# Seven products in another order, the root inside the squared ReLU, x transposed in the first group, merges by early transfers

## The chip, the cores and the metric

The kernel runs on one core of a Trainium2 chip, in one launch. The time is the device time of that core in microseconds; it is given as the median of several runs, with the lowest and the highest. Beside it there is one execution taken with the profiler. The engines are named as the profile names them: PE is TensorE (matmuls; PEld its weight loads), DVE is VectorE, ACT is ScalarE, POOL is GpSimd, SP is SyncE. Each takes its instructions strictly in the order in which they stand in its queue. SP issues plain transfers; POOL issues transfers that add to what is already at their destination ("accumulating transfers").

## The reference

A trunk of two layers on x of 512 tokens by 1024 features, in float32. Each layer has an attention part (not touched by the change) and an MLP with a squared ReLU; at the end stands a last norm:

```python
for l in range(DEPTH):                      # DEPTH = 2
    h = rmsnorm(x, attn_norm[l])
    ...                                     # two kinds of attention, one output projection w_o
    x = x + einsum('bse,ed->bsd', mixed, w_o[l])
    h = rmsnorm(x, mlp_norm[l])             # x * rsqrt(mean(x^2) + 1e-6) * g
    u = square(relu(einsum('bsd,df->bsf', h, w_ff1[l])))     # 1024 -> 4096
    x = x + einsum('bsf,fd->bsd', u, w_ff2[l])               # 4096 -> 1024
return rmsnorm(x, final_norm)
```

The norm's factor is one number per token, so it may be applied to the product with `w_ff1` rather than to x; and since it is positive, it may be applied after the squared ReLU as its square, 1 / (mean(x^2) + eps), which needs no root.

## The kernel before

**Precision.** Every float32 operand is split into a high part (rounded to the matmul's format) and a low part (the rest). A product takes three matmuls: high x high, high x low, low x high (`three`, L281 to L283). ACT makes the high part (L116 for weights, L224 for activations), DVE the low part (L117, L225). Weights come in units of 512 KB; `_Weights` loads them (SP, L99), splits them some units ahead and hands them out. While a layer's MLP runs, four split units are held.

**Layout.** x lies transposed, as 8 chunks of 128 features by 512 tokens. `h_hi`, `h_lo` are x times the norm's gain, split (`make_h`, L228 and L229); the sum of squares over the features is gathered in `ssq` (L235, L238) during the output projection `wo`.

**The MLP** of a layer runs in four groups of 1024 hidden features. A group first makes eight blocks of 128 hidden features (tiles `f`, 24 matmuls each, into PSUM banks that rotate over five). `evict_u` takes each block out of PSUM: ReLU (L810), square (L811), splits and, for two blocks together (a "pair"), the differences that the second half needs (L816, L819). The work tiles F hold one pair at a time.

The second half of a group multiplies with `w_ff2`. Two halves of the tokens, two of the hidden features and two of the output columns make a 2x2 by 2x2 block product; it is done with seven products instead of eight (a Strassen scheme), named in `FORMS`: "11", "21", "x1", "22", "x2", "x3", "x4", in this order. Each takes 24 matmuls into two PSUM banks, and `gather` (L833, L835) adds the result to a tile of its own, `y[form]`, over the four groups. The left operand of a form is one of seven splits of a pair (`SIDE`): 0 to 2 are quarters of u, 3 to 6 differences. The right operands are sums of quarters of `w_ff2` ("11", "12", "21", "22"). They are made in three buffers per unit by transfers: `fetch` loads a quarter (SP, L777), `grow` adds another to it (POOL, L783) as soon as the form that used the buffer before has been split; "11" becomes x1, x2 and x4 in turn, and "21" is replaced by "12" and grown by "22" to x3 (L782).

**The ends.** In the last group the seven tiles are combined into the four quarters of the result. `merge` (L843) adds one tile to another by an accumulating transfer on POOL's queue, `join` (L840) does it on DVE. In layer 0, `back` (L872, L873) transposes the result chunk by chunk on PE, adds it to x, and makes the next layer's h; the first two blocks of the next projection (tiles `p`) follow at once, then `p1w0v`. In the last layer the result stays with tokens in rows, so x is transposed the other way (`turned`, L852) and added; then come the sums of squares for the last norm (`square`, L878), its factor (`root`, L883 and L884), the gains (`weigh`, L888, and L896) and the stores (L894, L896, L898).

**The norm's factor in the MLP.** At the head of the first group the sum over features is made (L929, L930), and its reciprocal is held per token in `r2` (L934). It is applied at the very end: `settle` scales what has been combined so far (L862 on ACT in layer 0; L858 on DVE in the last layer, together with x), and `add_to` (L866) adds each late product scaled. `rms_a` and `rms_b`, which the attention uses for its own norms, make the root and spread it over a tile: PE transposes and DVE sums (L248 to L251), POOL takes the power -1/2 (L259), DVE makes the high and the low diagonal (L260 to L266), PE multiplies them with ones (L274, L275), ACT copies the result into `rbc` (L276).

**The order.** The program is written down in one order, and a scheduler places the instructions of each engine by priority; waits are put in from what reads and writes what. The order of an engine's queue is thus fixed before the run. Places such as `(g, k, n) == (0, 0, 6)` say after which matmuls something is written.

## Time and profile before

| | |
|---|---|
| time, median of 3 runs | 1177.74 us (1174.94 to 1179.62) |
| profiled execution, its own time | 1172.68 us |
| its span, first to last instruction | 1170.9 us |
| granted TensorE clock, mean | 0.998 |
| PE busy | 1147.6 us (98%) |
| DVE busy | 813.1 us (69%) |
| ACT busy | 651.5 us (56%) |
| POOL busy | 212.7 us (18%) |
| moved by DMA | 170.11 MB |

The MLP of layer 0 begins near 249 us and gives way to the next layer near 577; that of the last layer begins near 829. Durations of matmuls overlap (they are pipelined), so the distance of two starts, 0.227 us for 512 columns, is what one costs. On DVE too an instruction begins some 0.08 us before the end of the one ahead. A wait is shown in square brackets: the idle time before the instruction and what ended it. A busy time over a window stands in the order PE, PEld, DVE, ACT, POOL, with the number of instructions, then the granted clock, the DMA engines' share and GB/s.

### The profile page before, as it was taken

The page shows a single profiled execution, that of the slowest core. Times are in us where ns is not written, and L with a number is a line of the kernel's source. Part 1 is how long each engine was busy: PE and PEld are TensorE (multiplying, and loading weights), DVE is VectorE, ACT ScalarE, POOL GpSimd, SP SyncE. Part 2 cuts the span into 40 slices and gives each one's busy share as a digit, 9 for nine tenths or more (in the row PEclk, how much of TensorE's full clock was granted, in tenths as well). Part 3 has the DMA queues.
Part 4 walks back from the last instruction along what each step waited for, and adds up shares of the span by engine and source line. Part 5 has one row for each costly group of instructions (what it writes and reads, how often), then busy time and mean ns, then how long its engine had stood idle before and what let it go on. Part 6 is the DMA issues. An engine that isn't in the chain of part 4 may idle for free.

```text
span 1170.9 us, 15335 instructions
## 1 busy us (share of the span) xinstructions
PE 1147.6 (98%) x5454; PEld 951.2 (81%) x5454; DVE 813.1 (69%) x1302; ACT 651.5 (56%) x1153; POOL 212.7 (18%) x282
## 2 busy tenths in 40 slices
PE   9999999999999999999899999999999999999996
PEld 6787888888888888888677878888888888888885
DVE  7888788765545746647778887877664466475568
ACT  6455666556656446455445555655666564554554
POOL 1222443130100101002012215331201010010021
PEclk9999999999999999999999999999999999999999
DMA  7555333255844936727416553432548357276185
GB/s 243 158 156 172 119 116 108 72 189 153 196 149 108 229 123 125 222 96 159 106 54 190 153 161 109 125 110 72 216 120 224 128 127 228 93 148 210 36 175 132
DMA packets 56860, 170.11 MB, mean 145 GB/s; under 512 B 7120, under 2 KB 8144, under 8 KB 56784
## 3 DMA queue, kind: packets, MB, share of 16 engines
q1 hardware_dynamic: 46416, 131.88, 34.0%
q0 software_dynamic: 10224, 37.23, 18.0%
q8 instruction: 43, 0.70, 0.2%
q14 instruction: 33, 0.27, 0.1%
q10 hardware_dynamic: 144, 0.02, 0.0%
HBM read 138.17 MB, written 2.10 MB: 120 GB/s over the span
## 4 chain that ended last, share of the span: by engine, by line
PE 86%; DVE 5%; DMA 2%; issue 2%; ACT 1%; POOL 0%; SPq 0%; POOLq 0%; DVEq 0%; ACTq 0%
PE f L283 10%; PE f L281 10%; PE f L282 10%; PE x L281 4%; PE x L283 4%; PE x L282 4%; PE wo L281 3%; PE wo L283 3%; PE wo L282 3%; DMA q<-in_w 2%; DVE wlo L117 1%; PE T1s L555 1%; PE T0s L555 1%; PE O0s L584 0%; PE O1s L584 0%
## 5 line engine op out<-in xcount | busy, mean ns | idle before, releaser
L117 DVE TENSOR_TENSOR wlo<-raw,whi 128x1024 fp32r<-128x1024 f32 (+1 forms) x132 | 157.0, 1193 | 95.6 <-ACT whi L116 95.0
L117 DVE TENSOR_TENSOR wlo<-q,whi 128x512 fp32r<-128x512 f32 x224 | 145.9, 687 | 108.6 <-ACT whi L116 108.1
L281 PE MATMUL f<-h_hi,whi 128*128 128x512 f32 x512 | 199.6, 390 | 0.0
L283 PE MATMUL f<-h_hi,wlo 128*128 128x512 f32 x512 | 199.3, 389 | 0.0
L282 PE MATMUL f<-h_lo,whi 128*128 128x512 f32 x512 | 199.2, 389 | 0.0
L116 ACT ACTIVATE whi<-q 128x512 fp32r<-128x512 f32 x224 | 129.4, 624 | 123.7 <-DMA q<-in_w 45.4
L116 ACT ACTIVATE whi<-raw 128x1024 fp32r<-128x1024 f32 (+1 forms) x132 | 133.9, 1019 | 111.7 <-PE f L282 55.0
L783 POOL DMA_DIRECT2D q<-in_w x64 | 56.0, 882 | 557.1 <-DVE wlo L117 471.3
L283 PEld LDWEIGHTS f<-h_hi,wlo 128*128 128x128 f32 x512 | 96.1, 188 | 20.1
L282 PEld LDWEIGHTS f<-h_lo,whi 128*128 128x128 f32 x512 | 96.1, 188 | 20.0
L281 PEld LDWEIGHTS f<-h_hi,whi 128*128 128x128 f32 x512 | 96.1, 188 | 19.7
L225 DVE TENSOR_TENSOR Al<-F,Ah 128x256 fp32r<-128x256 f32 (+2 forms) x96 | 74.8, 779 | 44.1 <-ACT Ah L224 44.0
L281 PE MATMUL x<-whi,Ah 128*128 128x512 f32 x256 | 100.0, 391 | 0.0
L282 PE MATMUL x<-wlo,Ah 128*128 128x512 f32 x256 | 99.8, 390 | 0.0
L283 PE MATMUL x<-whi,Al 128*128 128x512 f32 x256 | 99.7, 389 | 0.0
L224 ACT ACTIVATE Ah<-F 128x256 fp32r<-128x256 f32 (+2 forms) x96 | 67.6, 704 | 45.7 <-DVE F L819 43.7
L282 PEld LDWEIGHTS x<-wlo,Ah 128*128 128x128 f32 x256 | 48.1, 188 | 10.3 <-DVE wlo L117 0.5
L283 PEld LDWEIGHTS x<-whi,Al 128*128 128x128 f32 x256 | 48.1, 188 | 10.0
L281 PEld LDWEIGHTS x<-whi,Ah 128*128 128x128 f32 x256 | 48.1, 188 | 9.8
L810 ACT ACTIVATE F<-f 128x512 f32<-128x512 f32 x64 | 37.5, 587 | 10.8 <-DVE Al L225 5.4
L811 ACT ACTIVATE F<-F 128x512 f32<-128x512 f32 x64 | 40.4, 631 | 1.5
L228 ACT ACTIVATE h_hi<-x,g_all 128x512 fp32r<-128x512 f32 x32 | 22.5, 718 | 26.6 <-DVE x L692 13.8
(1059 smaller groups left out, 2566.5 us busy)
## 6 DMA issues: line engine op xcount, KB each, us to landing
raw<-in_w SPq DMA_DIRECT2D x126, 512.0 KB, 3.6
q<-in_w SPq DMA_DIRECT2D x64, 512.0 KB, 5.5
q<-in_w POOLq DMA_DIRECT2D x64, 512.0 KB, 5.9
x<-in_xT SPq DMA_DIRECT2D x8, 256.0 KB, 4.6
raw<-in_w SPq DMA_DIRECT2D x8, 128.0 KB, 4.5
yx<-y POOLq DMA_DIRECT2D x2, 512.0 KB, 8.0
y<-y POOLq DMA_DIRECT2D x2, 512.0 KB, 7.5
y<-yx POOLq DMA_DIRECT2D x2, 512.0 KB, 5.3
```

What stands on the lines that cost most here:

```text
L116: h = nc.scalar.activation(hi[:, a:b], raw[:, a:b], AF.Copy)
L117: self.last = h, nc.vector.tensor_tensor(out=lo[:, a:b], in0=raw[:, a:b], in1=hi[:, a:b].bitcast(F32), op=ALU.subtract)
L224: nc.scalar.activation(hi, src, AF.Copy)
L225: nc.vector.tensor_tensor(out=lo, in0=src, in1=hi.bitcast(F32), op=ALU.subtract)
L228: a = nc.scalar.activation(h_hi[:, c, :], x[:, c, :], AF.Copy, scale=g)
L281: nc.tensor.matmul(pt, ah, bh, start=first, stop=False)
L282: nc.tensor.matmul(pt, ah, bl, start=False, stop=False)
L283: nc.tensor.matmul(pt, al, bh, start=False, stop=last)
L555: nc.tensor.transpose(pt[:, off : off + P], u["w"][qi][:, kb * P : (kb + 1) * P], ident)
L783: nc.gpsimd.dma_start(t, quad(g, q, c), accum_op=ALU.add)
L810: nc.scalar.activation(t, pt, AF.Relu)
L811: nc.scalar.activation(t, t, AF.Square)
```

## The change

- The forms run in the order "11", "x3", "x1", "22", "x2", "21", "x4". The buffer that held "21" first and x3 later now holds x3 first: a group ahead, "12" is loaded and "22" added to it; once x3 is split, "21" is loaded over it.
- The norm's factor is made as a root by `rms_a` and `rms_b` in the first two blocks of the first group, into `rbc`. `evict_u` takes a block out of PSUM with one DVE instruction that does the ReLU and multiplies by `rbc`; ACT's ReLU goes. The first block is held back until the second has been multiplied. `column`, `settle` and `add_to` go.
- In the last layer six of the eight transposes of x (`forth`, formerly `turned`) are written into the tiles `y` in the first group, and the forms "21", "22" and "x4" add to them from the start. The other two stand in the form x2 of the last group.
- In the last group "11" is merged into x2 and 21 at once, x3 into x4, x1 into x3, x1 into 22, by five transfers; x2 is then joined to x3, x4 and 22 on DVE, for both layers alike. The places of `back`, `square`, `root`, `weigh` and `store` follow.

```diff
--- before.py
+++ after.py
...
-FORMS = ("11", "21", "x1", "22", "x2", "x3", "x4")
+FORMS = ("11", "x3", "x1", "22", "x2", "21", "x4")
...
                 W.raw[unit(g, form, c)] = kept[k][c]
-                nc.sync.dma_start(kept[k][c], quad(g, form, c))
-
-            def grow(g, form, q, c, over=None):
+                nc.sync.dma_start(kept[k][c], quad(g, "12" if form == "x3" else form, c))
+                if form == "x3":
+                    nc.gpsimd.dma_start(kept[k][c], quad(g, "22", c), accum_op=ALU.add)
+
+            def grow(g, form, q, c):
                 t = kept[HOME[form]][c]
-                if over:
-                    nc.sync.dma_start(t, quad(g, over, c))
-                nc.gpsimd.dma_start(t, quad(g, q, c), accum_op=ALU.add)
+                if q == form:
+                    nc.sync.dma_start(t, quad(g, q, c))
+                else:
+                    nc.gpsimd.dma_start(t, quad(g, q, c), accum_op=ALU.add)
...
                             ("11", grow, (g, "x1", "12", c)), ("x1", grow, (g, "x2", "22", c)),
-                            ("x2", grow, (g, "x4", "21", c)), ("21", grow, (g, "x3", "22", c, "12")),
-                            ("x4", fetch, (g + 1, "11", c)), ("x3", fetch, (g + 1, "21", c)),
+                            ("x2", grow, (g, "x4", "21", c)), ("x3", grow, (g, "21", "21", c)),
+                            ("x4", fetch, (g + 1, "11", c)), ("21", fetch, (g + 1, "x3", c)),
...
                             W.then.setdefault(unit(g, form, c), []).append(lambda fn=fn, args=args: fn(*args))
-            for form in ("11", "21", "22"):
+            for form in ("11", "x3", "22"):
             def evict_u(pt, g, k, forms):
...
                 t = F[:, 2 * which : 2 * which + 2, :].rearrange("p a t -> p (a t)")
-                nc.scalar.activation(t, pt, AF.Relu)
+                nc.vector.scalar_tensor_tensor(out=t, in0=pt, scalar=0.0, in1=rbc, op0=ALU.max, op1=ALU.mult)
...
                     split(hi[:, 0, :], lo[:, 0, :], F[:, 1, :])
...
-            fresh = set(FORMS)
-            home = {(1, 0): "21", (1, 1): "22", (0, 0): "x4", (0, 1): "z" if last else "x1"}
+            fresh = set(FORMS) - ({"21", "22", "x4"} if last else set())
+            home = {(1, 0): "21", (1, 1): "22", (0, 0): "x4", (0, 1): "x3"}
...
                 return y[home[(tb // 2, j)]][:, tb % 2, :]
...
-            def column(tb):
-                return r2[:, tb : tb + 1]
-
-            def turned(tb, j):
+            def forth(tb, j):
...
                     nc.tensor.transpose(pt[:, k * P : (k + 1) * P], x[:, 4 * j + k, tb * P : (tb + 1) * P], ident)
-                return pt
-
-            def settle(tb, j):
-                o = place(tb, j)
-                if last:
-                    nc.vector.scalar_tensor_tensor(
-                        out=o, in0=o, scalar=column(tb), in1=turned(tb, j), op0=ALU.mult,
-                        op1=ALU.subtract if j else ALU.add)
+                if (tb // 2, j) == (0, 1):
+                    nc.vector.tensor_sub(place(tb, j), place(tb, j), pt)
                 else:
-                    nc.scalar.activation(o, o, AF.Copy, scale=column(tb))
-
-            def add_to(tb, j, src):
-                o = place(tb, j)
-                nc.vector.scalar_tensor_tensor(
-                    out=o, in0=src, scalar=column(tb), in1=o, op0=ALU.mult, op1=ALU.add)
+                    nc.scalar.activation(place(tb, j), pt, AF.Copy, scale=-1.0 if j else 1.0)
...
-            r2 = fin[:, 0:4]
+            def diagonals():
+                f = fp.tile([P, 4, S], F32R, tag="F", name=f"diag{l}")
+                parts_ = iter((f[:, 0, :], f[:, 1, :]))
+                return lambda name: next(parts_)
+
...
                 end = g == GROUPS - 1
...
                     nc.scalar.activation(sin_t, sin_t, AF.Copy, scale=-math.sqrt(D))
+                waiting = []
...
                         if (g, k, n) == (0, 0, 6):
-                            ptr = bank("t", f"rs_m{l}")
-                            for j in range(4):
-                                nc.tensor.transpose(ptr[:, j * P : (j + 1) * P], ssq[:, j * P : (j + 1) * P], ident)
-                            nc.vector.tensor_reduce(
-                                out=r2, in_=ptr.rearrange("p (j f) -> p j f", j=4), axis=AX.X, op=ALU.add)
-                            nc.vector.tensor_scalar(
-                                out=r2, in0=r2, scalar1=1.0 / D, scalar2=EPS, op0=ALU.mult, op1=ALU.add)
-                            nc.vector.reciprocal(r2, r2)
-                    evict_u(pt, g, k, forms)
-                    if end and k in (2, 3):
-                        settle(k - 2, 0)
+                            dg = rms_a(ssq, 1.0 / D, rcol, f"m{l}", nc.vector, diagonals())
+                        if (g, k, n) == (0, 1, 4):
+                            rms_b(rbc, f"m{l}", dg)
+                    waiting.append((pt, k))
+                    if (g, k) == (0, 0):
+                        continue
+                    for one, i in waiting:
+                        evict_u(one, g, i, forms)
+                    waiting = []
+                    if last and g == 0 and k < 7:
+                        forth(*((2, 0), (3, 0), (2, 1), (3, 1), (0, 0), (1, 0))[k - 1])
...
                     work = [(c, i, r) for c in range(GP // 2) for i in range(2) for r in range(2)]
...
                               n == mine[0], n == mine[-1])
-                        if end and last and form == "x3" and n == 3:
-                            join("22", "x2")
-                            for tb in (2, 3):
-                                settle(tb, 1)
-                                square(tb, 1)
-                                root(tb)
-                                weigh(tb, 0)
+                        if end and last and form == "x2" and n in (1, 3):
+                            forth(n // 2, 1)
                         if tail and last and n == 3:
-                            add_to(0, 0, to[0])
+                            gather("x4", to, (0,))
                             square(0, 0)
-                            weigh(2, 1)
-                            weigh(3, 1)
                             root(0)
                             for tb in (2, 3):
-                                for j in range(2):
-                                    store(tb, j, True)
-                        if tail and not last and n == 5:
-                            for c_ in CAME[:2]:
+                                weigh(tb, 0)
+                                store(tb, 0, True)
+                                store(tb, 1, True)
+                        if tail and not last and n in (3, 5, 7):
+                            for c_ in ((4,), (5, 6), (7,))[n // 2 - 1]:
...
                         break
-                    if end and not last and form == "x3":
-                        for tb in (0, 1):
-                            add_to(tb, 1, to[tb])
...
                         merge("x2", "11")
-                    elif form == "21":
                         merge("21", "11")
+                    elif form == "x3":
+                        merge("x4", "x3")
+                    elif form == "x1":
+                        merge("x3", "x1")
                     elif form == "22":
                         merge("22", "x1")
-                        for tb in (2, 3):
-                            settle(tb, 0)
-                        if last:
-                            for tb in (2, 3):
-                                square(tb, 0)
-                            y["z"], t = (e.rearrange("p (a t) -> p a t", a=2) for e in kept[2])
-                            for tb in (0, 1):
-                                nc.scalar.activation(place(tb, 1), turned(tb, 1), AF.Copy, scale=-1.0)
-                                nc.scalar.activation(t[:, tb, :], y["x1"][:, tb, :], AF.Copy, scale=column(tb))
-                            y["t"] = t
-                            merge("z", "t")
                     elif form == "x2":
                         join("x3", "x2")
-                        if not last:
-                            join("x1", "x3")
-                            join("22", "x2")
-                            for tb in range(4):
-                                settle(tb, 1)
-                    elif form == "x3":
+                        join("x4", "x2")
+                        join("22", "x2")
                         if last:
                             for tb in (0, 1):
-                                add_to(tb, 1, y["x3"][:, tb, :])
                                 square(tb, 1)
-                        for tb in (0, 1):
-                            add_to(tb, 0, y["x3"][:, tb, :])
+                            for tb in (0, 1):
+                                weigh(tb, 1)
+                    elif form == "21" and last:
+                        for j in (1, 0):
+                            for tb in (2, 3):
+                                square(tb, j)
+                        for tb in (2, 3):
+                            root(tb)
+                            weigh(tb, 1)
             if last:
-                add_to(1, 0, to[1])
+                gather("x4", to, (1,))
                 square(1, 0)
                 store(0, 0, False)
-                weigh(0, 1)
                 store(0, 1, True)
-                weigh(1, 1)
...
                 store(1, 1, True)
...
                 pts = [bank("mm", f"p{l + 1}{i}") for i in range(2)]
-                for tb in (0, 1):
-                    add_to(tb, 0, to[tb])
-                for c in CAME[2:4]:
-                    back(c)
+                gather("x4", to)
```

## The prediction

> **What bounds the kernel now.** I read the page's parts 1 and 4, then busy time by stage, then TensorE's own waits.
>
> ```profile
> span 1170.9 us, 15335 instructions
> PE 1147.6 (98%) x5454; PEld 951.2 (81%) x5454; DVE 813.1 (69%) x1302; ACT 651.5 (56%) x1153; POOL 212.7 (18%) x282
> PE 86%; DVE 5%; DMA 2%; issue 2%; ACT 1%; POOL 0%; SPq 0%; POOLq 0%; DVEq 0%; ACTq 0%
> ...
> 252.00:333.00 81.00, 81.00 (x361) 67.06 (x360) 44.23 (x65) 51.03 (x80) 8.27 (x9) 1.00 0.72 206
> 496.00:577.00 81.00, 79.35 (x349) 64.89 (x348) 49.98 (x74) 43.78 (x70) 9.62 (x11) 1.00 0.54 122
> 577.00:600.00 23.00, 19.52 (x97) 15.10 (x98) 21.97 (x32) 11.74 (x18) 0.13 (x2) 1.00 0.17 60
> 1076.00:1171.00 95.00, 84.11 (x386) 69.23 (x384) 61.60 (x95) 49.12 (x86) 12.65 (x16) 0.98 0.50 115
> ...
> PE xT L852 <- DVE y L858: 2.6, 1, 2.6
> PE yT L872 <- DVE x L873: 1.9, 1, 1.9
> ```
>
> The window rows give, after the stretch, its length and the busy times of PE, PEld, DVE, ACT, POOL. TensorE is busy 81.00 of 81 us in an MLP group: nothing taken from another engine there is worth anything. In the MLPs time is lost in two places only, both at the end of a layer: 577 to 600 (and the 1.65 ahead of it), where DVE is busy 21.97 of 23 us, and the last group, where TensorE lacks 10.9 of 95 us, 8.2 of them behind its last matmul.
>
> **The change part by part.** The profiled execution took 1172.68 us, its span 1170.9; the median of the runs shown is 1177.74, 5.06 above. The sum is made against the former and carried over to the median.
>
> **The root at the head of each MLP (a cost).** The old reciprocal was needed late. Now rms_a and rms_b run in the first two blocks, and the two matmuls of rms_b stand in TensorE's order after five products of the second block.
>
> ```profile
> 256.51 0.69 DVE L930 TENSOR_REDUCE fin<-rs_m 128x4 f32<-128x512 f32 x1
> 258.29 0.39 PE L281 MATMUL f<-h_hi,whi 128*128 128x512 f32 x1
> 260.53 0.60 ACT L810 ACTIVATE F<-f 128x512 f32<-128x512 f32 x1 [2.69 <-PE f L283]
> 601.08 0.69 DVE L249 TENSOR_REDUCE ms<-rs_a 128x4 f32<-128x512 f32 x1 [0.99 <-PE rs_a L248]
> 602.06 1.04 POOL L259 TENSOR_TENSOR rcol<-ms,mhalf 128x4 f32<-128x4 f32 x1 [1.15 <-DVE ms L251]
> 604.05 0.69 DVE L266 TENSOR_TENSOR dgla<-edge,clo 128x512 fp32r<-128x512 f32 x1
> 608.85 0.59 ACT L276 COPY rbc<-rb_a 128x512 f32<-128x512 f32 x1 [4.39 <-PE rb_a L275]
> ```
>
> The same chain at the attention's head goes from reduction to second diagonal in 604.05 + 0.69 - 601.08 = 3.66 us. Here the reduction starts at 256.51 (the weight splits ahead of it on DVE are unchanged), so the diagonal is there at 260.17. TensorE, in order, arrives at 258.29 and goes on after the second matmul (0.23, the distance of two matmuls) at 260.4: +2.1 per layer, **+4.2** for two. The lower bound is 0.9, the four matmuls alone; the upper 6.7, if one more wide DVE instruction (1.23, as at 380.51 below) gets into each chain. The factor is then copied (0.59) by about 261.4, while the second block ends 2.1 after its old eviction at 260.53: the first pair is late only by TensorE's own shift. The power goes ahead of the accumulating transfers on POOL's queue; their weights are needed only after eight blocks of 24 matmuls.
>
> **The ReLU on DVE (nothing).**
>
> ```profile
> L810 ACT ACTIVATE F<-f 128x512 f32<-128x512 f32 x64 | 37.5, 587 | 10.8 <-DVE Al L225 5.4 <-PE f L283 5.4
> L413 DVE SCALAR_TENSOR_TENSOR t1s0q<-p1s0q,rbc x1: 692/692/692, 678.7 to 678.7; 128x512 f32<-128x512 f32 x1
> 374.57 0.39 PE L281 MATMUL 11010_3748<-whi,Ah 128*128 128x512 f32 x1
> 375.20 0.69 DVE L117 TENSOR_TENSOR wlo<-q,whi 128x512 fp32r<-128x512 f32 x1 [2.56 <-ACT whi L116]
> 380.51 1.23 DVE L225 TENSOR_TENSOR Al<-F,Ah 128x1024 fp32r<-128x1024 f32 x1
> ```
>
> ACT loses 37.5 us; DVE gains 64 x 0.69 = 44, 5.5 per group, and goes from 50 to 56 of 81 us. TensorE hides it. The tight place is the product now second, "x3": it needs the differences of the last pair, which "21" did not. Products take 24 matmuls, 5.44 us; the last pair of the second is wanted at 374.57 + 5.44 + 18 x 0.227 = 384.1. Its low part is ready at 380.51 + 1.23 = 381.7, and the new instruction falls into DVE's 2.56 idle ahead of it. Slack 2.4 us; with that cover gone, eight groups would pay each microsecond eight times.
>
> **Transposes of x (a cost).**
>
> ```profile
> 1153.48 1.04 PE L852 MATMUL xT<-edge,x 128*128 128x128 f32 x8
> 1154.27 0.47 PE L281 MATMUL x<-whi,Ah 128*128 128x512 f32 x1
> ```
>
> Eight take 0.79, 0.1 each. Six sets of four go into the last layer's first group, where TensorE has no room: +2.4. Two sets leave the last group's blocks: -0.8. **+1.6**, bounds 1.4 and 2.6 (four at 0.66 where they follow a wait).
>
> **The weights and the merges.** SP's queue keeps its order and count: "x3" and "21" change places. POOL's has two transfers more in layer 0, one more in layer 1, and the two accumulations for "x3" move into the group before.
>
> ```profile
> 546.05 0.86 POOL L783 DMA_DIRECT2D q<-in_w  x1 [1.59 <-DMA q<-in_w]
> 546.61 1.19 POOL L843 DMA_DIRECT2D yx<-y  x1
> 549.18 0.88 POOL L783 DMA_DIRECT2D q<-in_w  x1 [1.38 <-DVE y L835]
> 552.04 0.87 POOL L843 DMA_DIRECT2D y<-y  x1 [1.97 <-issue]
> 554.56 0.86 POOL L783 DMA_DIRECT2D q<-in_w  x1 [1.65 <-DVE yx L835]
> ...
> 543.21 0.39 PE L281 MATMUL 21030_5022<-whi,Ah 128*128 128x512 f32 x1
> ...
> 549.18 8.43 DMA q<-in_w
> 563.63 5.32 DMA q<-in_w
> ```
>
> A lone transfer lands 5.3 after its issue (last line); in a backlog one follows another at some 2.65 (issues at 549.18, 552.04, 554.56) and takes 8.43. The second accumulation for x2 lands at 549.18 + 8.43 = 557.6 now and about 557 then: two merges are ahead of it in place of one merge and x3's accumulation. From there, 2.65 each: x3 into x4 559.5; x4's first weights 562.2; x1 into x3, which on POOL waits until x3 into x4 has landed, 559.6 + 5.3 = 564.9; x4's second 567.5; x1 into 22, 570.2. DVE's order puts the three joins, and in layer 1 two subtractions of x ahead of them, in front of the second half of x4's last weight split. That half is done 2.7 after the last merge (a join and a half of it queued, then the half): 572.9. TensorE begins x4, the seventh product, at 543.21 + 5 x 5.44 = 570.4 and wants the half 18 matmuls on, at 574.5: slack 1.6. In layer 1 x4's halves of tokens come one after the other, so on the same clock it is wanted at 573.5, and two multiplications by the gain (1.2) are ahead of it too: done at 574.4, a wait of 0.9 that I expect to see there.
>
> [...]
>
> **The end of layer 0 (a gain).**
>
> ```profile
> 575.49 1.40 DVE L866 SCALAR_TENSOR_TENSOR yx<-x,fin,yx 128x512 f32<-128x512 f32 x2
> 576.81 1.27 DVE L835 TENSOR_TENSOR yx<-yx,x 128x512 f32<-128x512 f32 x2
> 592.73 3.88 DVE L238 TENSOR_TENSOR ssq<-ssq,spare 128x512 f32<-128x512 f32 x5 [0.29 <-ACT spare L237]
> 597.80 0.50 PE L283 MATMUL p1w0v<-h_hi,wlo 128*128 128x512 f32 x1 [1.17 <-DVE wlo L117]
> ```
>
> DVE is the bound there. Six scaled additions (L866) go, of which pairs start 576.81 - 575.49 = 1.32 apart: -4.0, and two plain ones of x4 take the place of two of x3 before. One more addition to `ssq` (0.78) now stands ahead of the split for which TensorE waits at 597.80. **-3.2**, bounds 0 (the joins come late) and -5.1 (all that TensorE lacks in the two windows, 1.65 + 3.48).
>
> **The end of the kernel (a gain).**
>
> ```profile
> 1145.02 0.66 PE L852 MATMUL xT<-edge,x 128*128 128x128 f32 x4 [2.61 <-DVE y L858]
> 1162.33 0.39 PE L283 MATMUL x<-whi,Al 128*128 128x512 f32 x1
> 1166.37 0.75 DVE L896 SCALAR_TENSOR_TENSOR yx<-yx,fin,cos_t 128x512 f32<-128x512 f32 x1 [0.66 <-POOL fin L884]
> ```
>
> The wait of 2.61 goes: the two sets left there find their banks free. But the last store comes 4.0 after the last matmul, off DVE's queue. On that, from x2's additions on, two L858 and six L866 go (8 x 0.66 = 5.3); one join of 1024 (1.14), two additions of x4 and two multiplications by the gain (4 x 0.6) come: **-1.8**. Bounds 0 and -3.8, the shift of TensorE's last matmul.
>
> Sum: 4.2 + 0 + 1.6 - 3.2 - 1.8 = +0.8: 1173.5 for the profiled execution, **1178.5** beside the median. 0.5%, 5.9 us, is about what a measurement can tell.
>
> **The rivals.**
> *Merges late (slower).* Five merges per layer instead of three or four, DVE waits for the last two, and the split of x4's weights stands behind them. For it: the queue is full in the rows above; POOL is blocked while x1 into x3 waits. Against: two accumulations leave this stretch. From 1.6 late it costs both layers; from 3.4 late it decides (1.8 in layer 0, 3.4 in layer 1, on top of +0.8: 6.0). Two transfers late, 5.3: 3.7 + 5.3 + 0.8 = +9.8, **1187.5**. Chance 0.2.
>
> *Both ends relieved (faster).* DVE had 21.97 of 23 us; without the scalings TensorE could run through: 4.2 + 1.6 - 5.1 - 3.8 = -3.1; with roots as early as their bound, -6.4: **1171.3**. Against it: 3.66 us of chain can't fit in 258.29 - 256.51. Chance 0.1.
>
> *Nothing hidden, nothing gained.* The second product waits for its differences and the new order costs what the ends give. From 2.4 late; at 3 late 8 x 0.6 = 4.8: 1183.3. Against it: the 2.56 idle. Chance 0.04.
>
> *The clock falls.*
>
> ```profile
> 1140.00:1150.00 10.00, 7.39 (x41) 6.01 (x40) 8.11 (x14) 6.91 (x15) 2.60 (x3) 1.00 0.93 173
> 1163.00:1171.00 8.00, 0.00 (x0) 0.00 (x0) 3.46 (x6) 2.85 (x6) 1.10 (x2) 0.76 0.51 197
> ```
>
> The granted clock (after POOL's column) stays 1.00 over an idle of 2.61 and is 0.76 over one of 8. My waits at the roots are 1.7; twice that, and then half speed for as long, would be 2 x 3.4 = +6.8 on the sum: 1185.3. Chance 0.03. [...]
>
> **How the numbers follow.** The forecast, within 0.5%, holds 0.63. Slower is merges 0.2 and clock 0.03; faster 0.1; the late differences lie inside. That leaves 0.67 for the same. The range, 1173 to 1187, leaves out most of the faster case and the worst of the merges; the likeliest case alone spans 1174 to 1183.
>
> **What the profile after would show.** TensorE waiting about 1.7 us at rms_b in both layers; no wait above 0.3 within groups; L813 64 times at 0.69; no ACT wait of 7 us on a transfer (L862 is gone) but DVE waits on merges in the last groups; the TensorE waits of 577 to 600 mostly gone; the last matmul some 3 us earlier against the start of its group, the last store about 2. Wrong I would be if the joins or the roots came a transfer later than reckoned, or if TensorE lost time in groups 1 to 3.

## The result, and the profile after

The changed kernel takes 1180.16 us (median of 13 runs, 1177.94 to 1182.32), the kernel before, run beside it, 1175.15 us (13 runs, 1173.54 to 1179.62). The ratio is 1.0038, its 95% interval 1.0027 to 1.0049: 4.5 us slower, a small but measured loss, inside the half per cent that I called no change. The forecast of 1178.5 lies close, but its sum does not: it stood on a median of 1177.74 of three runs, and said +0.8 where +4.5 was measured.

The profiled execution of the changed kernel took 1180.27 us, near its own median; that of the kernel before, 1172.68, lies 2.5 below its median. So the two profiles differ by 7.5 us in their spans. That is what is accounted for below; where part of the 2.5 comes from is shown with the experiments.

From the page of the changed kernel, span and busy time:

```profile
span 1178.4 us, 15339 instructions
PE 1152.0 (98%) x5458; PEld 953.3 (81%) x5458; DVE 852.4 (72%) x1367; ACT 611.0 (52%) x1079; POOL 219.8 (19%) x287
```

TensorE's busy time grew by 4.4 us for four more matmuls: some matmuls got longer. Its waits (total, times, longest), and busy time by stage (columns as before: PE, PEld, DVE, ACT, POOL, granted clock, DMA share, GB/s):

```profile
PE rb_m L274 <- DVE diag L264: 4.6, 2, 2.4
PE yT L861 <- DVE x L862: 2.4, 1, 2.4
...
PE x L282 <- DVE wlo L117: 0.9, 1, 0.9
```

```profile
252.00:333.00 81.00, 78.82 (x342) 64.55 (x342) 49.13 (x74) 44.24 (x70) 11.66 (x12) 0.98 0.74 196
833.00:915.00 82.00, 79.58 (x357) 65.18 (x356) 50.34 (x77) 45.21 (x73) 12.69 (x13) 0.98 0.67 181
333.00:415.00 82.00, 82.00 (x363) 67.92 (x362) 54.57 (x81) 39.13 (x59) 6.94 (x8) 1.00 0.61 157
577.00:600.00 23.00, 19.42 (x98) 14.91 (x96) 20.88 (x31) 11.48 (x18) 0.13 (x2) 1.00 0.15 46
```

The first groups of both MLPs, full at clock 1.00 before, now lack 2.2 and 2.4 us and run at 0.98; the second group (third line) is full as before. TensorE's timeline gives the stages: the first block, the first "11" of the first and of the last group, the transposes for the next norm (`rs_a`), the last matmul. First the changed kernel, then the one before.

```profile
248.64 0.39 PE L281 MATMUL f<-h_hi,whi 128*128 128x512 f32 x1
...
260.27 0.47 PE L274 MATMUL rb_m<-diag,ones_r 128*128 128x512 f32 x1 [2.14 <-DVE diag L264]
260.78 0.79 PE L275 MATMUL rb_m<-diag,ones_r 128*128 128x512 f32 x1
261.37 0.63 PE L281 MATMUL f<-h_hi,whi 128*128 128x512 f32 x1
261.80 0.63 PE L282 MATMUL f<-h_lo,whi 128*128 128x512 f32 x1
...
264.95 0.39 PE L282 MATMUL f<-h_lo,whi 128*128 128x512 f32 x1
265.17 0.39 PE L283 MATMUL f<-h_hi,wlo 128*128 128x512 f32 x1
...
297.38 0.39 PE L281 MATMUL 11000_3142<-whi,Ah 128*128 128x512 f32 x1
...
542.18 0.39 PE L281 MATMUL 11030_4986<-whi,Ah 128*128 128x512 f32 x1
...
603.43 0.60 PE L248 MATMUL rs_a<-edge,ssq 128*128 128x128 f32 x4
...
832.25 0.39 PE L281 MATMUL f<-h_hi,whi 128*128 128x512 f32 x1
...
848.50 0.60 PE L852 MATMUL xT<-edge,x 128*128 128x128 f32 x4
848.85 0.48 PE L281 MATMUL f<-h_hi,whi 128*128 128x512 f32 x1
...
884.03 0.39 PE L281 MATMUL 11100_8324<-whi,Ah 128*128 128x512 f32 x1
...
1128.83 0.39 PE L281 MATMUL 11130_10166<-whi,Ah 128*128 128x512 f32 x1
...
1168.89 0.39 PE L283 MATMUL x<-whi,Al 128*128 128x512 f32 x1
```

```profile
248.95 0.39 PE L281 MATMUL f<-h_hi,whi 128*128 128x512 f32 x1
...
292.97 0.39 PE L281 MATMUL 11000_3132<-whi,Ah 128*128 128x512 f32 x1
...
537.77 0.39 PE L281 MATMUL 11030_4978<-whi,Ah 128*128 128x512 f32 x1
...
600.44 0.60 PE L248 MATMUL rs_a<-edge,ssq 128*128 128x128 f32 x4
...
829.13 0.39 PE L281 MATMUL f<-h_hi,whi 128*128 128x512 f32 x1
...
873.15 0.39 PE L281 MATMUL 11100_8279<-whi,Ah 128*128 128x512 f32 x1
...
1118.91 0.39 PE L281 MATMUL 11130_10133<-whi,Ah 128*128 128x512 f32 x1
```

The distances between these rows, in us (the last matmul before is at 1162.33, shown in the prediction):

| stretch | before | after | difference |
|---|---|---|---|
| head 0: first block to first "11", layer 0 | 44.02 | 48.74 | +4.72 |
| groups, layer 0: first "11" to last "11" | 244.80 | 244.80 | 0 |
| end 0: last "11" to `rs_a` | 62.67 | 61.25 | -1.42 |
| head 1, last layer | 44.02 | 51.78 | +7.76 |
| groups, last layer | 245.76 | 244.80 | -0.96 |
| end 1: last "11" to last matmul | 43.42 | 40.06 | -3.36 |
| tail: last matmul to the end of the span | 8.57 | 9.51 | +0.94 |

With -0.18 for the rest this is the 7.5. What is lost is lost at the heads, but for 0.9 in the tail. At head 0 the wait of 2.14 is only half: behind it the matmuls start 0.43 apart (261.37, 261.80) instead of 0.23 (264.95, 265.17), and the granted clock (the third number from the end) says why:

```profile
257.26:260.68 3.42, 1.28 (x5) 0.56 (x3) 2.48 (x5) 0.00 (x0) 1.86 (x1) 1.00 1.03 400
260.68:264.09 3.41, 3.37 (x9) 2.63 (x9) 0.74 (x2) 1.63 (x3) 1.98 (x2) 0.50 1.02 417
264.09:267.50 3.41, 3.41 (x17) 2.78 (x16) 2.22 (x4) 1.26 (x2) 0.00 (x0) 1.00 1.00 303
```

Head 0 is so 44.02 + 2.14 (wait) + 0.48 (the two matmuls, measured below without a wait) + 2.10 (what the wait brings behind it: a restart, and the half clock). In head 1 a set of transposes takes 0.45: 0.35 to the next matmul (848.50 to 848.85) and 0.10 on the two distances behind it; six take 2.7. That leaves 2.42 (wait) + 0.48 + 2.2 (behind the wait). Of the 2.1 and 2.2 some 0.6 are my estimate of the restart, from what is left over in mid_root below at full clock; the half clock is the other 1.5 or so, by seven distances of 0.43 instead of 0.23.

### The profile page after: what moved, and what is told of

Its sections match the earlier page's. It is cut to its first block, busy times and chain, and to the rows that moved or that the text cites. A ratio compares the mean times of both kernels' runs of the same rounds, so it can differ in the third digit from the quotient of the medians.

```text
span 1178.4 us, 15339 instructions
## 1 busy us (share of the span) xinstructions
PE 1152.0 (98%) x5458; PEld 953.3 (81%) x5458; DVE 852.4 (72%) x1367; ACT 611.0 (52%) x1079; POOL 219.8 (19%) x287
## 3 DMA queue, kind: packets, MB, share of 16 engines
q0 software_dynamic: 10656, 38.80, 18.8%
## 4 chain that ended last, share of the span: by engine, by line
PE 82%; DVE 6%; DMA 3%; issue 3%; POOL 2%; ACT 1%; SPq 0%; POOLq 0%; DVEq 0%; ACTq 0%
PE f L281 9%; PE f L283 9%; PE f L282 9%; PE x L281 4%; PE x L283 4%; PE x L282 4%; PE wo L281 2%; PE wo L282 2%; PE wo L283 2%; DMA yx<-yx 2%; DVE wlo L117 1%; DMA q<-in_w 1%; PE T1s L555 1%; PE T0s L555 1%; PE O0s L584 0%
## 5 line engine op out<-in xcount | busy, mean ns | idle before, releaser
L786 POOL DMA_DIRECT2D q<-in_w x48 | 42.3, 882 | 485.2 <-DVE wlo L117 475.4
L282 PEld LDWEIGHTS f<-h_lo,whi 128*128 128x128 f32 x512 | 96.8, 189 | 20.1
L225 DVE TENSOR_TENSOR Al<-F,Ah 128x256 fp32r<-128x256 f32 (+2 forms) x96 | 74.7, 778 | 44.1 <-ACT Ah L224 43.9
L813 DVE SCALAR_TENSOR_TENSOR F<-f,rbc 128x512 f32<-128x512 f32 x64 | 44.1, 689 | 74.3 <-PE f L283 71.1
```

The lines of the kernel that those rows point to most:

```text
L225: nc.vector.tensor_tensor(out=lo, in0=src, in1=hi.bitcast(F32), op=ALU.subtract)
L282: nc.tensor.matmul(pt, ah, bl, start=False, stop=False)
L786: nc.gpsimd.dma_start(t, quad(g, q, c), accum_op=ALU.add)
L813: nc.vector.scalar_tensor_tensor(out=t, in0=pt, scalar=0.0, in1=rbc, op0=ALU.max, op1=ALU.mult)
```

## The experiments

All ratios are to the kernel before, run beside them, with the 95% interval.

**The root's place.**

```diff
-                        if (g, k, n) == (0, 1, 4):
+                        if (g, k, n) == (0, 2, 2):
                             rms_b(rbc, f"m{l}", dg)
...
-                    if (g, k) == (0, 0):
+                    if g == 0 and k < 2:
                         continue
...
-                    if last and g == 0 and k < 7:
-                        forth(*(...)[k - 1])
+                    if last and g == 0:
+                        forth(*(...)[k - 2])
```

> The changed kernel with one thing moved: the two matmuls of rms_b stand after the third product of the third block of the first group instead of after the fifth product of the second, and the first two blocks' evictions are held until then (the six transposes of x in the last layer move by one block with them). TensorE reaches the new place 3.8 us later (6 products of 0.68 less the overlap with the wait, from the distance of two matmuls, 0.227), after the second diagonal is there. Theory: the root's price is its wait (2.14 and 2.42 us in the profile of the changed kernel) plus the slow matmuls behind it (0.427 us apart instead of 0.227 for some 3 us, granted clock 0.50): both vanish, -9 us against the changed kernel in the profile (2.14 + 2.13 + 2.42 + 2.76), and the median lands near 1171 to 1173. Rival 1: the clock there falls because the DMA engines are full (share 1.0 in that stretch) and not because of the wait: only the waits vanish, -4.6, median near 1175.5. Rival 2: two blocks' evictions held back make the first product '11' late, and a wait at its head takes the place of the one removed: no change, 1180.

Measured: 1173.63 us (12 runs), ratio 0.9986 (0.9973 to 0.9999), 0.52% below the changed kernel's ratio, 6.1 us. The row of `rb_m` on TensorE:

```profile
262.75 0.40 PE L274 MATMUL rb_m<-diag,ones_r 128*128 128x512 f32 x1
```

It stands without a wait. Head 0 is 44.50 us, 0.48 over the kernel before: the root's bare price. The median lies just above the theory's 1171 to 1173; of its 9 us two thirds came. The clock stays at 1.00, though the DMA engines are as full as in the changed kernel (share 1.01 to 1.03 from 258 to 266 us): rival 1 falls. Head 1 is 48.14, with a wait of 0.7 in it for POOL's last addition to `ssq`. Rival 2 falls too: nothing waits for the evictions held back.

**The same, half way.**

```diff
-                        if (g, k, n) == (0, 1, 4):
+                        if (g, k, n) == (0, 1, 6):
```

> The changed kernel with the two matmuls of rms_b two products later (after the seventh product of the second block), nothing else. TensorE arrives 1.36 us later (two products of 0.68), so a wait of about 0.8 us is left in layer 0 and 1.05 in layer 1. Theory: a wait that short does not bring the slow clock; the matmuls behind it stay 0.227 apart: -(1.36 + 2.1) - (1.36 + 2.8) = -7.6 us against the changed kernel in the profile, median near 1172.5 to 1174. Rival 1 (slow clock after any wait, or from the full DMA engines): only 2.7 us are gained, median near 1177.5. Rival 2: the slow clock is shorter in the measure of the wait (half of it stays): -5, median near 1175.

Measured: 1177.49 us (12 runs), ratio 1.0011 (0.9995 to 1.0027), 3.2 us below the changed kernel. The waits were 1.32 and 1.06, and the clock behind them did not fall:

```profile
263.44 0.47 PE L274 MATMUL rb_m<-diag,ones_r 128*128 128x512 f32 x1 [1.32 <-DVE diag L264]
```

```profile
264.00:266.00 2.00, 2.00 (x9) 1.65 (x10) 0.89 (x2) 0.75 (x2) 0.78 (x2) 1.00 1.02 418
```

So the mechanism at the root is the theory's (no slow stretch behind these two waits), while the time is rival 1's: of the 7.6 expected 3.2 came. The theory put all of the 2.1 and 2.8 to the clock. Head 1, 48.99 us, shows what is left at full clock: over the 44.50 of late_root's head 0 it has 1.06 (wait), 2.8 (the six sets of transposes, 47.28 - 44.50 in late_joins, below) and 0.6 left over, which I count as the restart. The rows show 0.1 of such a one: behind the wait of 1.17 in the kernel before, the next matmul starts 0.34 on (597.80 to 598.14) instead of 0.23. In layer 0 TensorE also met a wait that the changed kernel's profile lacks (0.7 for the last addition to `ssq`, below). The two heads together are 4.3 shorter, and 3.0 of it is lost elsewhere in this profile, in part behind another fall of the clock near 600 us (last section).

**The other direction.**

```diff
-                        if (g, k, n) == (0, 1, 4):
+                        if (g, k, n) == (0, 1, 2):
```

> The changed kernel with the two matmuls of rms_b two products earlier (after the third product of the second block): TensorE arrives 1.36 us sooner, and its waits at the root grow from 2.14 and 2.42 to about 3.5 and 3.8. Theory A (behind a wait of about 2 us or more the clock is halved for a stretch of a set length, some 3 us, whatever the wait): the slow stretch stays as it was and only the waits grow, +2.7 us against the changed kernel in all, median near 1183. Theory B (the slow stretch grows with the wait): another 2 us or more on that, 1185 or later. Theory C (it is a matter of chance and not of the wait): the slow stretch is missing in one of the layers, about 1180.

Measured: 1181.88 us (9 runs), ratio 1.0044 (1.0026 to 1.0061), 0.7 us above the changed kernel by the ratios. The edit did less than I meant: the scheduler moved only the first of the two matmuls, by one matmul and not six, and the waits became 2.89 and 2.65. Seven matmuls or so behind each start 0.43 apart, in both layers again. The clock's record decides between A and B: it is at 0.50 for 3.41 us behind both, as it was behind the waits of 2.14 and 2.42 in the changed kernel. That is A, a set length; what C (chance) has of truth is said in the last section.

**Merges as joins.**

```diff
-                        merge("x4", "x3")
+                        join("x4", "x3")
...
-                        merge("x3", "x1")
+                        join("x3", "x1")
```

> The changed kernel with x3 into x4 and x1 into x3 added on DVE (join) instead of by accumulating transfers (merge): POOL's queue has two transfers less in each layer's last group, DVE two instructions of 1024 columns (1.2 us each) more, written where the merges stood. Theory (the queue makes x4's second weights late, and DVE stands 3.50 us in front of their split with the three joins queued behind it): those weights land about 3 us earlier, DVE's first addition in back comes as much earlier, TensorE's wait of 2.40 us there goes in layer 0, the wait of 0.95 in the last product of layer 1 and DVE's wait of 3.00 on x1 into x3 go too: -2 to -4 us against the changed kernel, median 1176 to 1178. Rival (DVE is the bound of both ends, and 2.4 us more work on it costs what the queue gives): within 0.5 of the changed kernel or up to 2 slower, 1180 to 1182. The price of the root is not touched: TensorE's waits at rms_b stay 2.1 and 2.4.

Measured: 1179.59 us (12 runs), ratio 1.0036 (1.0021 to 1.0051): as good as no change in the median. But its stages did change: end 0 59.40 (61.25 in the changed kernel), end 1 38.80 (40.06), tail 8.82 (9.51), 3.8 us in all, while the heads, with waits of 2.65 and 2.64, took 2.4 more. The joins, which stand in the last group, did not do that: at both heads TensorE first waits 0.7 for the last addition to `ssq`, and the root's chain comes later with it (last section). DVE's rows at the end of layer 0, first in the changed kernel, then here:

```profile
573.77 0.69 DVE L117 TENSOR_TENSOR wlo<-q,whi 128x512 fp32r<-128x512 f32 x1 [3.50 <-ACT whi L116]
...
581.85 0.68 DVE L862 TENSOR_TENSOR x<-x,yT 128x512 f32<-128x512 f32 x1
583.32 0.75 DVE L229 SCALAR_TENSOR_TENSOR h_lo<-x,g_all,h_hi 128x512 fp32r<-128x512 f32 x1 [0.79 <-ACT h_hi L228]
...
592.65 0.68 DVE L862 TENSOR_TENSOR x<-x,yT 128x512 f32<-128x512 f32 x1
```

```profile
573.12 0.69 DVE L117 TENSOR_TENSOR wlo<-q,whi 128x512 fp32r<-128x512 f32 x1 [0.68 <-ACT whi L116]
...
581.20 0.68 DVE L862 TENSOR_TENSOR x<-x,yT 128x512 f32<-128x512 f32 x1
```

Counted from the last "11" (542.18 and, here, 543.41) the first addition of `back` comes at 39.67 and 37.79: the wait for x4's last weights shrinks from 3.50 to 0.68, and 1.9 us come through to `rs_a`. Whether that counts in the median had to be tried without the heads' waits:

```diff
 # late_root and joins_dve together
```

> late_root and joins_dve together. In the profile of joins_dve the stretches at the ends were shorter than in that of late_root: 59.40 against 60.56 us from the last group's first product to the next layer's rs_a, 38.80 against 40.22 in the last layer's products, 8.82 against 9.58 behind the last matmul, 3.3 in all, while its median lay only 0.6 below the changed kernel's. Theory (the queue of merges does cost 3 us, and the heads' slow clock hid it): 1173.6 - 3.3 = about 1170.3. Rival (the ends' gain is a matter of one profile, DVE is the bound): 1173 to 1174, no change from late_root.

Measured: 1169.85 us (6 runs), ratio 0.9947 (0.9927 to 0.9967): 0.39% or 4.6 us below late_root, the intervals apart. The queue of merges does cost time: the theory's 3.3 us lie well inside the noise of the 4.6.

```diff
-                        if tail and not last and n in (3, 5, 7):
-                            for c_ in ((4,), (5, 6), (7,))[n // 2 - 1]:
+                        if tail and not last and n in (5, 7):
+                            for c_ in ((4, 5), (6, 7))[n // 2 - 2]:
...
-                        if (g, k, n) == (0, 0, 6):
+                        if (g, k, n) == (0, 1, 0):
...
-                        if (g, k, n) == (0, 2, 2):
+                        if (g, k, n) == (0, 2, 4):
```

> late_joins with two more moves: back takes chunks 4 and 5 after the sixth product of x4 and 6 and 7 after the last (in pairs, as the kernel before did) instead of 4, then 5 and 6, then 7; and the root's two places move by 1.4 us (rms_a into the second block, rms_b behind the fifth product of the third), so that TensorE does not meet POOL's last addition to ssq, on which it waited 0.7 us in some of the profiles. Theory: the pairs take back the 1.0 us that DVE lost between the first and the last addition in back (10.8 us against 9.8 before), the root 0 to 0.7 a layer: 1 to 2 below late_joins, near 1169. Rival: the first chunk comes 1.4 us later and DVE is the bound all the same: no change or up to 1 slower than late_joins.

Measured: 1167.35 us (6 runs), ratio 0.9929 (0.9909 to 0.9950): 8.3 us faster than the kernel before, the fastest of all, and 2.1 below late_joins by the ratios, whose intervals overlap. The end of layer 0 in its profile, with TensorE busy 21.80 of 23 us:

```profile
577.00:600.00 23.00, 21.80 (x108) 17.36 (x107) 19.21 (x31) 11.63 (x19) 1.80 (x7) 1.00 0.18 67
```

End 0 is 57.81, against 58.71 in late_joins: the pairs give 0.9, where 1.0 was expected. The root's later places gave nothing in this profile: instead of 0.7 for `ssq`, TensorE waits 1.0 for the last `h_lo` in each head (45.78 and 48.55 us).

**The ReLU, in the old order.**

```diff
-                nc.scalar.activation(t, pt, AF.Relu)
+                nc.vector.tensor_scalar(out=t, in0=pt, scalar1=0.0, scalar2=None, op0=ALU.max)
```

> The kernel before with one thing changed: the ReLU that takes a block out of PSUM is a maximum with 0 on DVE instead of an activation on ACT (64 instructions). Theory (hidden behind TensorE, which is busy 81 of 81 us in a group): no change, within 1 us of the kernel before, groups 1 to 3 still 81.6 us from one product '11' to the next. Rival: DVE's added 44 us push a split past its due time: each group longer by what is late, +2 us or more in all.

Measured: 1179.36 us (12 runs), ratio 1.0034 (1.0017 to 1.0050). Neither case: the groups take 81.60 us as ever, yet 4.0 us are lost. Its profile is 6.0 longer than that of the kernel before: 3.7 of them at end 0 (66.41 us), 1.7 at the two heads. At the end the transfers that make x2's weights come later: on POOL's queue their second accumulation is issued 13.4 us after the last "11" (551.83 against 538.45) where it was 11.4 (549.18 against 537.77), and the one for x4 behind it 20.1 against 16.8 (558.55, 554.56). DVE's split of x2's weights comes 2.5 later, and TensorE waits where it did not:

```profile
565.15 0.51 PE L281 MATMUL x<-whi,Ah 128*128 128x512 f32 x1 [2.06 <-ACT whi L116]
```

```profile
586.00:590.00 4.00, 3.93 (x12) 2.83 (x11) 3.69 (x6) 1.34 (x2) 0.00 (x0) 0.58 0.13 54
```

The clock falls behind this wait (0.57 from 565 to 569 us) and behind the next (0.58 in the last row). That DVE's added work pushes them fits these rows, but which transfer first lost its place was not settled.

**The ReLU, in the new order.**

```diff
-                            dg = rms_a(ssq, 1.0 / D, rcol, f"m{l}", nc.vector, diagonals())
...
-                            rms_b(rbc, f"m{l}", dg)
...
-                nc.vector.scalar_tensor_tensor(out=t, in0=pt, scalar=0.0, in1=rbc, op0=ALU.max, op1=ALU.mult)
+                nc.vector.tensor_scalar(out=t, in0=pt, scalar1=0.0, scalar2=None, op0=ALU.max)
```

> The changed kernel without the root: rms_a and rms_b are left out, so the MLP's result is not scaled by the norm's factor; the eviction is a maximum with 0 on DVE, at once. It leaves the order of forms, the transposes and the merges as they are. Theory (all that the root costs beyond late_root is its eight transposes and four matmuls, 2 x (0.36 + 0.48) = 1.7): 1173.6 - 1.7 = about 1172, and -8 against the changed kernel. Rival (holding the first two evictions back costs something by itself in late_root): below 1171.

```diff
+                nc.scalar.activation(t, pt, AF.Relu)
```

> noroot_dve (the norm's factor left out) with the ReLU back on ACT. Theory (the ReLU on DVE costs nothing in the new order, whose accumulations for x3 lie a group earlier): within 1 us of noroot_dve. Rival (as in relu_before, where DVE's added work put the accumulating transfers of the last group up to 3.3 us later and the median 4.6 us higher): 2 to 4 us below noroot_dve.

Measured: 1171.36 us (12 runs), ratio 0.9966 (0.9953 to 0.9980), and 1170.34 us (7 runs), ratio 0.9955 (0.9936 to 0.9974). In both the first block is still held back until the second is done. The first lies 8.5 us below the changed kernel: the whole price of the root in the median, of which late_root gets back 6.1. Between the two lies 1.0 us, inside their intervals: in the new order, whose accumulations for x3 lie a group earlier, no cost of the ReLU beyond DVE's time is seen. The intervals do not exclude one of 2 or 3 us, so that the order is what makes the difference to the old one is likely, not shown.

**The transposes of x.**

```diff
-            fresh = set(FORMS) - ({"21", "22", "x4"} if last else set())
+            fresh = set(FORMS)
...
-                    if last and g == 0:
-                        forth(*(...)[k - 2])
```

> late_root without the six transposes of x in the last layer's first group; the three tiles that they fill start from the first product instead, so six quarters of x are left out of the result. Theory (each set of four costs TensorE 0.36 us, by the distance of the starts in the profile of the changed kernel, 848.50 to 848.85): -2.1 us against late_root, median near 1171.5, the stretch from the last layer's first block to its first product '11' down from 48.1 to 46.0. Rival (TensorE has room for them, as the head's waits come anyway): no change. My own price of 0.1 for each transpose would give -2.4.

Measured: 1171.17 us (6 runs), ratio 0.9951 (0.9932 to 0.9970): 2.5 us below late_root by the medians, 4.1 by the ratios, whose intervals lie just apart. Head 1 falls from 48.14 to 44.50 us, the very value of head 0 in late_root. 3.6 is more than the theory's 2.1: six sets are 2.7, and late_root had a wait of 0.7 there. The rival falls.

**The kernel before, once more.**

> The kernel before, unchanged, for a second profile of it: its profiled execution (1172.68) lay 2.5 us below its median. Theory (what varies is the end of layer 0 and the clock there): from the last group's first product to the next layer's rs_a it takes 62.7 us or up to 4 us more, with a granted clock below 1.00 where it is more; groups and attention agree within 0.3 us. Rival: the heads of the MLPs or the attention vary as much.

Measured: 1174.51 us (10 runs), ratio 0.9997 (0.9977 to 1.0016), its span 1172.6 against 1170.9. My theory named the wrong place: end 0 took 62.76 (62.67 before), end 1 45.28 (43.42). The last group's wait of 2.61 is 2.86 here, and this time the clock falls behind it (a line of the kernel's text more shifts the line numbers by one):

```profile
1145.10 0.66 PE L853 MATMUL xT<-edge,x 128*128 128x128 f32 x4 [2.86 <-DVE y L859]
```

```profile
1142.40:1145.81 3.41, 0.71 (x5) 0.63 (x6) 3.41 (x7) 1.76 (x5) 0.87 (x1) 1.00 0.90 157
1145.81:1149.22 3.41, 3.41 (x11) 2.84 (x11) 2.30 (x4) 1.70 (x4) 0.87 (x1) 0.50 0.82 159
```

So in one of its two profiles the kernel before pays for its own wait; that its profile on record was free of it explains part of the 2.5 us to its median.

## Why the prediction was right, and where not

The case that I held likeliest came: a change inside half a per cent, head and transposes against the two ends. That 1178.5 lies so near to 1180.16 is partly luck: the sum of +0.8 on the median of 1175.15 gives 1176.0, and the three runs that it was put on lay 2.6 higher. The sum missed by 6.7 us in the profile. By its terms:

- *Roots, +4.2.* Measured 9.8 (0.96 for the matmuls, 4.56 waiting, 4.3 behind the waits, some 3 of them from the half clock). This is the step that failed, in two ways. The wait was 2.1 and 2.4 instead of 1.7, because "the same chain at the attention's head" is not the same: the power took 1.96 us instead of 1.04, beside a split that DVE does at that moment (last section). And the clock fell behind waits of 2.1 to 2.4. I had that as a rival at a chance of 0.03, on the ground of one idle stretch of 2.61 behind which the clock stayed at 1.00. Another profile of the same kernel shows that stretch, 2.86 long, with a fallen clock: one row of one execution could not carry that exclusion. Waits at the root of 3.4, which the rival's sum took, no run shows: they were 2.14 to 2.89, with the clock at 0.50 for 3.41 us behind each.
- *ReLU, 0.* In the new order nothing speaks against it: groups of 81.60 us, 64 instructions of 0.69 (44.1 us in all), 1.0 us in the pair without the root, inside the noise. Wrong as a general statement, as the old order shows, and there it cost what my argument did not look at: not TensorE's cover in the groups, but the accumulating transfers of the last one.
- *Transposes, +1.6.* Measured 2.7 - 0.96 = +1.7. The price of 0.1 for each was nearly right because 0.35 and the restart behind it make 0.45 for four.
- *Weights and merges.* The landing times held within about 1 us. x4's last weights, reckoned at 567.5, landed at 573.0 with the whole layer 4.4 later, so 1.1 late. The wait of 0.9 that I expected in the last layer stood there, 0.95, and there was none in layer 0. My working for the 0.9 does not come out, though: 572.9 and the 1.2 that it adds are 574.1, not 574.4, and leave 0.6.
- *End of layer 0, -3.2.* Measured -1.42. Here the saving on DVE did not come through. Its first addition in `back` moved by as much as reckoned, the last by less. The kernel before:

```profile
580.46 1.28 DVE L873 TENSOR_TENSOR x<-x,yT 128x512 f32<-128x512 f32 x2
...
590.22 0.68 DVE L873 TENSOR_TENSOR x<-x,yT 128x512 f32<-128x512 f32 x1
```

  From the last "11" (537.77) these are 42.69 and 52.45; in the changed kernel 39.67 and 50.47. 3.0 became 2.0, since the first chunk now goes alone and DVE waits 0.79 for ACT's high part; the additional addition to `ssq` took 0.8 as reckoned, and some 0.2 came back behind it. Pairs gave 0.9 back. Before all this DVE had stood 3.50 us for x4's weights with the three joins queued behind: what I counted as saved work was in part exchanged for waiting.
- *End of the kernel, -1.8.* Measured -2.4. The last matmul came 3.36 earlier against the start of its group ("some 3"), but the tail grew by 0.9. I put that down to the joins, which run late on DVE there; that was not tried by itself.

Of the signs, one failed plainly: TensorE's waits from 577 to 600 were not mostly gone (3.48 us before, 3.58 after). And no sign named a change of clock.

## What to carry to other kernels

A wait of TensorE is not paid by its length alone: price it with the restart and the half clock that may follow (at head 0 of the changed kernel the wait of 2.14 brought 2.10 more), and put what it waits for a few matmuls later, where a later place costs nothing (here 6 us for moving two matmuls). A chain that is copied from another place has that place's neighbours in its durations (the power took 1.96 us where 1.04 was copied): look at what the second engine does beside each link before taking them over. Where accumulating transfers make the next operands, an instruction added to the engine that releases their buffers can cost time even where TensorE hides it in the groups (4.0 us in the old order).

## What the runs showed of the hardware

*The clock.* In the thirteen profiles TensorE has 54 waits of 0.9 to 1.75 us after its start, and the matmuls slow down behind none of them. Of 21 waits of 1.88 to 3.12 us the clock fell behind 11: behind all 6 at the root (2.14 to 2.89), and behind 5 of the 15 others, among which one of 1.88 brought it and one of 3.12 did not. Then some seven matmuls start 0.43 apart; at the root of the changed kernel about 2.1 us are lost so, the restart included.

When the clock falls says more than the length of the wait. By the clock's record each of these falls lasts 3.41 us, and within a profile they begin a whole number of times 3.413 us apart: at 260.68 and 844.36 in the changed kernel (171 times), at 263.34, 584.19 and 847.01 in early_root (94 and 77 times). So I laid stretches of 3.413 us through each profile, counted from its falls, and took TensorE's busy time in each; that the clock is set by such stretches is a guess that nothing here tried by itself. In the changed kernel's rows above the stretch ahead of the fall has TensorE busy for 1.28 us, in before_again for 0.71. In the kernel before a border of the stretches lies in the middle of the wait of 2.61 (at 1143.27, seven stretches ahead of its one fall, at 1167.16, behind its last matmul). The stretch ahead of the border has TensorE busy for 2.56 us, the one behind it for 1.66, and the clock stays:

```profile
1143.27:1146.68 3.41, 1.66 (x12) 1.49 (x13) 3.41 (x6) 1.76 (x5) 0.87 (x1) 1.00 0.94 175
```

In the stretches ahead of the 11 falls TensorE was busy for 0.71 to 1.54 us. Up to the last matmul no stretch behind which the clock stayed at 1.00 had it busy for less than 1.53. One more fall does not fit, in mid_root behind waits of only 0.56 and 0.73:

```profile
597.36:600.77 3.41, 2.03 (x7) 0.81 (x6) 3.20 (x5) 2.31 (x3) 0.00 (x0) 1.00 0.00 0
600.77:604.18 3.41, 3.41 (x9) 2.64 (x9) 1.47 (x2) 0.00 (x0) 0.63 (x4) 0.50 0.65 198
```

So neither the length of a wait nor this busy time parts all the falls from the rest. How one wait can cost in one run and not in the next is not shown; my guess is its place among the stretches: the wait of 2.61 lies across two of them, while that of 2.86 in before_again lies in one but for its first 0.2 us. Ahead of the six falls at the root TensorE was busy for at most 1.50 us. Other executions of the changed kernel seem to be spared: its six fastest runs, 1177.94 to 1178.86 us, have a mean granted clock of 0.996 or 0.997, the profiled one 0.994.

*POOL beside DVE.* The power at the root, with DVE's split of weights beside it, in the changed kernel (DVE, then POOL), and in late_joins_back, where three splits are done ahead of the reduction and none beside the power:

```profile
257.02 1.22 DVE L117 TENSOR_TENSOR wlo<-raw,whi 128x1024 fp32r<-128x1024 f32 x1
...
257.16 1.96 POOL L259 TENSOR_TENSOR rcol<-ms,mhalf 128x4 f32<-128x4 f32 x1 [4.37 <-DVE ms L251]
```

```profile
254.75 3.70 DVE L117 TENSOR_TENSOR wlo<-raw,whi 128x1024 fp32r<-128x1024 f32 x3 [0.57 <-ACT whi L116]
...
259.33 1.02 POOL L259 TENSOR_TENSOR rcol<-ms,mhalf 128x4 f32<-128x4 f32 x1 [5.70 <-DVE ms L251]
```

It took 1.96 in both layers of the seven other kernels that have the root, and 1.02 in both layers here: 0.9 us of each root's chain. The kernel before had shown it: its first power, at 25.16 us beside a split of DVE at 25.11, took 2.06. Why the power takes longer beside a split these rows do not show. The 0.7 to 1.0 that TensorE waits at the head of some profiles looks like the same: where POOL's addition to `ssq` takes 1.3 or 1.4 us, DVE's `h_lo` beside it takes 1.76 instead of 0.74, and the root's reduction comes later (257.66 in joins_dve, 256.19 in the changed kernel). That was not tried by itself.
